# Low parts of block sums on the vector engine, low parts of gate weights by DMA, and all pairs normalized before the first evacuation

## The chip, the cores and the metric

The kernel runs on one core of one Trainium2 chip. Time is device microseconds (us) of that core, from the runs' times; the profile is one further execution with a time of its own. Engines are named as in the profile: PE is the matrix engine (PEld its weight load), DVE the vector engine, ACT the scalar engine, POOL the general engine (it issues the accumulating DMAs), SP the engine that issues the weight loads. Each engine works through its own list of instructions in a fixed order.

## The reference

Two layers over a sequence of 512 positions with 1024 channels, in float32. Layer 0 mixes with a gated convolution and a causal pooling, layer 1 with a spatial gating; each is followed by the same gated ConvFFN, and it is at the start of that FFN, in both layers, that the change lies.

```python
def rms_norm(x, g):
    x32 = x.astype(jnp.float32)
    y = x32 * lax.rsqrt(jnp.mean(x32 * x32, axis=-1, keepdims=True) + EPS)
    return y.astype(x.dtype) * g

def gated_conv_ffn(x, w_gate, w_up, conv_w, conv_b, w_down):
    g = jnp.einsum('bsd,df->bsf', x, w_gate)
    g = causal_dwconv3(g, conv_w) + conv_b
    up = jnp.einsum('bsd,df->bsf', x, w_up)
    return jnp.einsum('bsf,fd->bsd', jax.nn.silu(g) * up, w_down)
...
        hn = rms_norm(h, norm_ffn[layer])
        h = h + gated_conv_ffn(hn, w_ffn_gate[layer], w_ffn_up[layer], conv_ffn[layer],
                               b_conv_ffn[layer], w_ffn_down[layer])
```

The hidden width is 2816, that is 22 columns of 128; the convolution is causal and three wide.

## The kernel before, in words

*Arithmetic.* Every float32 operand of a product is split into a high part that PE takes (float32r) and a low part, the rest. A product is three matmuls into one PSUM bank (`mm3`, lines 134 to 137): high by high, high by low, low by high. A high part is a copy on ACT. A low part is made in one of two ways: `parts` (127 to 132) subtracts on DVE; `summed` (118 to 125) writes the negated high part on ACT, and a DMA issued by POOL adds the source to it (lines 122 to 124).

*Layout.* The residual h lies transposed: eight blocks of 128 channels by 512 positions (`h[0]` to `h[7]`), and beside it `hg`, a high and a low part of each block, the moving operand of the FFN. `PAIRS` sets the order in which the blocks are used: 0, 4, 1, 5, 2, 6, 3, 7. Pair kp is the blocks kp and kp + 4.

*The FFN's groups.* `Ffn.hidden` goes through the 22 columns two at a time; I call two columns a group. The first group (f = 0, `direct`) multiplies with `hg` as it was before normalization (only scaled by the gain), since the norm's root isn't known yet; its results are multiplied by the root r later, in its evacuation. While PE works on it, r becomes known (`rstd_tokens`, `rstd_spread`), and `normalize(kp)` rewrites `hg` for one pair at a time:

- x (line 571, DVE): both blocks of h times gain times r;
- the high parts (575, ACT) and low parts (576, DVE) of the two blocks of hg;
- t (583 to 586, DVE, 256 wide): four block sums of x, which the later groups need for their seven products;
- the split of t into high and low in two halves (590 to 593), by the way of `summed`: ACT, POOL's DMA, ACT.

x and t take turns in three buffers of one tag ("sum"); a buffer is free when all readers of its tile are done, DMAs among them. The weight sums of the later groups (s23, s14) use the same three.

The second group (f = 2, also `direct`) uses the normalized hg: first both gate columns over the eight blocks, then both up columns. From the third group (f = 4, `seven`) on, the up part is seven half-wide products of block sums (line 660, tiles ua, ue, ub) between the gate products (g). Line 617 splits its weight sums.

*Evacuation.* The first group's evacuation (`evacuate`, 547 to 562) multiplies the gate by r on DVE (555), does the convolution (504 on ACT, 506 twice on DVE), silu on ACT (512), a product with r on POOL (558), the product with the up part on DVE (561) and the split of the result (261, 263).

*Loads.* Weights come through four raw buffers in turn (tag "raw", 512 KB each); SP issues the next load when the buffer's last readers are done. The parts have five buffers each (tags "whi", "wlo"), and a buffer is rewritten when PE has used it.

*What sets the order.* The program is written in the order of `hidden`: for the first group, the group's own matmuls, then `pair_weights` of the second group, `normalize` of pairs 0 to 2, the evacuation (`rest`), and `normalize` of pair 3 (lines 717 to 723). A scheduler then places the instructions of each engine by this order and by its own estimate of when operands are ready, so neighbours on an engine may be interleaved. The lists of all engines are fixed when the kernel is built.

Of the kernel before, what the change touches and what calls it, by code (L numbers as in the profile page):

```python
# [15 lines left out]
P = 128  # L16
# [14 lines left out]
def tile_trunk(ctx: ExitStack, tc: tile.TileContext, x, norm_mix, norm_ffn, final_norm,  # L31
# [95 lines left out]
    def parts(raw, a, b, name):  # L127
        hi = wp.tile([P, a, b], F32R, tag="whi", bufs=5, name=f"whi_{name}")
        lo = wp.tile([P, a, b], F32R, tag="wlo", bufs=5, name=f"wlo_{name}")
        nc.scalar.activation(hi, raw, AF.Copy)  # L130
        nc.vector.tensor_tensor(lo, raw, hi.bitcast(F32), ALU.subtract)  # L131
        return hi, lo
# [344 lines left out]
    NP = NK // 2  # L477
# [9 lines left out]
    class Ffn:  # L487
# [27 lines left out]
        def act(self, ft, s):  # L515
            self.acts[ft] = split(self.ap, s, f"a{self.layer}_{ft}", tag="a", bufs=6)

        def pair_weights(self, f, order):

            ch = {}  # L520
            for key, half in order:
                name = f"{key}{self.layer}_{f}_{half}"
                raw = wp.tile([P, 4, 2 * P], F32, tag="raw", bufs=4, name=f"raw_{name}")
                w = (w_ffn_gate if key == "g" else w_ffn_up)[self.layer][:, f * P : (f + 2) * P]
                w = w.rearrange("(h k p) c -> p h k c", h=2, p=P)
                for h_ in range(2):
                    nc.sync.dma_start(raw.rearrange("p (k h) c -> p h k c", h=2)[:, h_],
                                      w[:, h_, 2 * half : 2 * half + 2])
                ch[key, half] = parts(raw, 4, 2 * P, name)
            return ch  # L530

        def direct(self, f, normed, sets, ch, before=lambda i, j: None):
# [33 lines left out]
        def normalize(self, kp):  # L566

            n, r = f"{self.layer}_{kp}", self.r
            x = self.ap.tile([P, 2, S], F32, tag="sum", bufs=3, name=f"x{n}")
            for i, k in enumerate((kp, kp + NP)):  # L570
                nc.vector.scalar_tensor_tensor(x[:, i, :], h[k], self.prm("ffn", k), r,
                                               op0=ALU.mult, op1=ALU.mult)

            def halves(dst, src):
                nc.scalar.activation(dst[0], src, AF.Copy)
                nc.vector.tensor_tensor(dst[1], src, dst[0].bitcast(F32), ALU.subtract)

            halves(hg[kp], x[:, 0, :])
            halves(hg[kp + NP], x[:, 1, :])
            b11, b12 = x[:, 0, :HALF], x[:, 0, HALF:]  # L580
            b21, b22 = x[:, 1, :HALF], x[:, 1, HALF:]
            t = self.ap.tile([P, 4, HALF], F32, tag="sum", bufs=3, name=f"t{n}")
            nc.vector.tensor_tensor(t[:, 1, :], b22, b12, ALU.subtract)
            nc.vector.tensor_tensor(t[:, 0, :], t[:, 1, :], b11, ALU.add)
            nc.vector.tensor_tensor(t[:, 3, :], b12, b11, ALU.subtract)
            nc.vector.tensor_tensor(t[:, 2, :], b21, t[:, 0, :], ALU.subtract)
            self.t23[kp] = self.sums(kp)
            t41 = self.ap.tile([P, 2, 2, HALF], F32R, name=f"t41_{n}")
            self.t41[kp] = t41[:, 0], t41[:, 1]
            for (hi, lo), src in ((self.t23[kp], t[:, :2, :]), (self.t41[kp], t[:, 2:, :])):  # L590
                nc.scalar.activation(lo, src, AF.Copy, scale=-1.0)
                nc.gpsimd.dma_start(lo, src, accum_op=ALU.add)
                nc.scalar.activation(hi, src, AF.Copy)
# [114 lines left out]
        def hidden(self, f, before=lambda i, j: None):  # L708
            if f == 0:
                def first(i, j):  # L710
                    before(i, j)
                    if (i, j) == (1, 0):
                        self.norm.rstd_tokens()
                    elif (i, j) == (2, 2):
                        self.r = self.norm.rstd_spread()

                ch = self.pair_weights(0, [("g", 0), ("u", 0), ("g", 1), ("u", 1)])
                rest = self.direct(0, False, (range(4),), ch, first)
                self.ch = self.pair_weights(2, [("g", 0), ("g", 1), ("u", 0), ("u", 1)])
                for kp in range(NP - 1):  # L720
                    self.normalize(kp)
                rest()
                self.normalize(NP - 1)
            elif f == 2:
                self.direct(2, True, ((0, 1), (2, 3)), self.ch)()
            else:
                self.seven(f)
# [264 lines left out]
```

## Time and profile before

| | |
|---|---|
| time, median of 3 runs | 1026.82 us (1026.61 to 1027.18) |
| profiled execution: its own time | 1027.26 us |
| its span | 1025.5 us |
| mean granted PE clock | 0.993 |
| PE busy | 1005.2 us, 98% |
| DVE busy | 611.0 us, 60% |
| ACT busy | 472.2 us, 46% |
| POOL busy | 91.8 us, 9% |

The span runs from the first to the last instruction; the execution's own time has 1.8 us around it. A line of a timeline gives start, duration, engine, line of the code, operation, output and inputs, and in brackets the idle time of the engine before it with what ended it. Instructions of one engine overlap at their ends, so the distance of two starts, not the duration, says what one more of a kind costs. PEclk is the share of its full clock that PE was granted.

### The profile page before, as it was taken

The page shows a single profiled execution, that of the slowest core. Times are in us where ns is not written, and L with a number is a line of the kernel's source. Part 1 is how long each engine was busy: PE and PEld are TensorE (multiplying, and loading weights), DVE is VectorE, ACT ScalarE, POOL GpSimd, SP SyncE. Part 2 cuts the span into 40 slices and gives each one's busy share as a digit, 9 for nine tenths or more (in the row PEclk, how much of TensorE's full clock was granted, in tenths as well). Part 3 has the DMA queues.
Part 4 walks back from the last instruction along what each step waited for, and adds up shares of the span by engine and source line. Part 5 has one row for each costly group of instructions (what it writes and reads, how often), then busy time and mean ns, then how long its engine had stood idle before and what let it go on. Part 6 is the DMA issues. An engine that isn't in the chain of part 4 may idle for free.

```text
span 1025.5 us, 13018 instructions
## 1 busy us (share of the span) xinstructions
PE 1005.2 (98%) x5169; PEld 857.4 (84%) x5169; DVE 611.0 (60%) x878; ACT 472.2 (46%) x689; POOL 91.8 (9%) x105
## 2 busy tenths in 40 slices
PE   9999999899999999999999999989999999999996
PEld 6788888688898889889888888878889988998885
DVE  5997556855556455636833645486645564664566
ACT  5423435641544246336655443575424632660553
POOL 3141121200000000000300001121000000000000
PEclk9999999899999999999999999999999999999999
DMA  7432234452444343524343223254425343543432
GB/s 228 157 103 82 83 107 106 117 142 64 126 127 138 82 124 116 150 64 139 117 136 103 67 98 94 72 123 106 144 64 139 108 140 82 139 118 93 120 87 82
DMA packets 79881, 114.99 MB, mean 112 GB/s; under 512 B 4069, under 2 KB 53453, under 8 KB 79821
## 3 DMA queue, kind: packets, MB, share of 16 engines
q1 hardware_dynamic: 73580, 98.96, 31.0%
q0 software_dynamic: 4896, 13.63, 7.4%
q10 hardware_dynamic: 1344, 1.58, 0.5%
q8 instruction: 40, 0.66, 0.3%
q14 instruction: 21, 0.16, 0.0%
HBM read 98.42 MB, written 2.10 MB: 98 GB/s over the span
## 4 chain that ended last, share of the span: by engine, by line
PE 92%; DVE 3%; ACT 2%; DMA 1%; issue 1%; POOL 0%; DVEq 0%; ACTq 0%; POOLq 0%
PE ua L660 10%; PE g L136 6%; PE g L135 6%; PE g L137 6%; PE ue L660 5%; PE d L136 4%; PE d L137 4%; PE d L135 4%; PE dn L136 4%; PE dn L137 4%; PE dn L135 4%; PE ub L660 3%; PE gu L136 2%; PE gu L137 2%; PE gu L135 2%; PE v L135 1%
## 5 line engine op out<-in xcount | busy, mean ns | idle before, releaser
L135 PE MATMUL g<-hgh,whi_g 128*128 128x512 f32 x288 | 112.5, 391 | 0.0
L136 PE MATMUL g<-hgl,whi_g 128*128 128x512 f32 x288 | 112.5, 391 | 0.0
L137 PE MATMUL g<-hgh,wlo_g 128*128 128x512 f32 x288 | 112.1, 389 | 0.0
L130 ACT ACTIVATE whi_g<-raw_g 128x1024 fp32r<-128x1024 f32 x44 | 46.3, 1053 | 93.6 <-PE dn L137 57.3
L131 DVE TENSOR_TENSOR wlo_g<-raw_g,whi_g 128x1024 fp32r<-128x1024 f32 x44 | 53.7, 1221 | 28.3 <-ACT whi_g L130 28.3
L136 PE MATMUL d<-a_lo,whi_d 128*128 128x512 f32 x176 | 68.6, 390 | 0.0
L135 PE MATMUL dn<-whi_dn,a_hi 128*128 128x512 f32 x176 | 68.6, 390 | 0.0
L136 PE MATMUL dn<-wlo_dn,a_hi 128*128 128x512 f32 x176 | 68.5, 389 | 0.0
L137 PE MATMUL d<-a_hi,wlo_d 128*128 128x512 f32 x176 | 68.5, 389 | 0.0
L137 PE MATMUL dn<-whi_dn,a_lo 128*128 128x512 f32 x176 | 68.3, 389 | 0.0
L135 PE MATMUL d<-a_hi,whi_d 128*128 128x512 f32 x176 | 68.3, 390 | 0.0
L123 POOL DMA_DIRECT2D wlo_u<-raw_u x18 | 15.4, 857 | 547.3 <-ACT wlo_u L122 261.5
L506 DVE SCALAR_TENSOR_TENSOR c<-rows,prm,c 128x512 f32<-128x512 f32 x88 | 63.7, 747 | 0.7
L137 PEld LDWEIGHTS g<-hgh,wlo_g 128*128 128x128 f32 x288 | 54.1, 188 | 11.9 <-DVE wlo_g L131 0.5
L135 PEld LDWEIGHTS g<-hgh,whi_g 128*128 128x128 f32 x288 | 54.2, 188 | 10.3
L136 PEld LDWEIGHTS g<-hgl,whi_g 128*128 128x128 f32 x288 | 54.2, 188 | 9.8
L617 DVE TENSOR_TENSOR wlo_a<-raw_u,whi_a 128x512 fp32r<-128x512 f32 x18 | 12.4, 691 | 82.1 <-ACT whi_a L616 82.1
L678 ACT COPY kept<-ua 128x256 f32<-128x256 f32 x54 | 19.8, 367 | 77.9 <-PE ua L660 77.9
L131 DVE TENSOR_TENSOR wlo_dn<-raw_dn,whi_dn 128x1024 fp32r<-128x1024 f32 x22 | 26.9, 1223 | 37.0 <-ACT whi_dn L130 37.0
L131 DVE TENSOR_TENSOR wlo_d<-raw_d,whi_d 128x1024 fp32r<-128x1024 f32 x22 | 26.9, 1222 | 37.0 <-ACT whi_d L130 37.0
L616 ACT ACTIVATE whi_s<-s 128x1024 fp32r<-128x1024 f32 x36 | 38.1, 1058 | 22.9 <-PE d L136 14.2
L921 DVE TENSOR_TENSOR y<-dn,y 128x512 f32<-128x512 f32 x32 | 22.1, 690 | 42.9 <-PE dn L137 42.9
(319 smaller groups left out, 2763.0 us busy)
## 6 DMA issues: line engine op xcount, KB each, us to landing
raw_u<-in_w_ffn_up_dram SPq DMA_DIRECT2D x36, 512.0 KB
raw_g<-in_w_ffn_gate_dram SPq DMA_DIRECT2D x36, 512.0 KB
raw_d<-in_w_ffn_down_dram SPq DMA_DIRECT2D x22, 512.0 KB
raw_dn<-in_w_ffn_down_dram SPq DMA_DIRECT2D x22, 512.0 KB
wlo_u<-raw_u POOLq DMA_DIRECT2D x18, 512.0 KB, 4.5
raw_oe<-in_w_out_even_dram SPq DMA_DIRECT2D x8, 512.0 KB
raw_g<-in_w_ffn_gate_dram SPq DMA_DIRECT2D x16, 256.0 KB
raw_u<-in_w_ffn_up_dram SPq DMA_DIRECT2D x16, 256.0 KB
```

Of the source, the lines that this page charges most:

```text
L123: nc.gpsimd.dma_start(lo, raw, accum_op=ALU.add)
L130: nc.scalar.activation(hi, raw, AF.Copy)
L131: nc.vector.tensor_tensor(lo, raw, hi.bitcast(F32), ALU.subtract)
L135: nc.tensor.matmul(ps, lhs[0], rhs[0], start=start, stop=False)
L136: nc.tensor.matmul(ps, lhs[0], rhs[1], start=False, stop=False)
L137: nc.tensor.matmul(ps, lhs[1], rhs[0], start=False, stop=stop)
L506: nc.vector.scalar_tensor_tensor(c, t[:, i : S + i], prm("cf", i * NF + ft), c, op0=ALU.mult, op1=ALU.add)
L616: nc.scalar.activation(hi, src, AF.Copy)
L617: nc.vector.tensor_tensor(lo, src, hi.bitcast(F32), ALU.subtract)
L660: nc.tensor.matmul(ps, l, r, start=at not in opened, stop=end, skip_group_check=True)
L678: nc.scalar.copy(kept[:, i, :], ps)
L921: nc.vector.tensor_tensor(dst, ps, dst, ALU.add)
```

## The change

Three edits, all in the start of an FFN, so each acts twice (once in each layer):

- `pair_weights` can take the way of `summed` for chosen keys; for the second group's gate weights it does. Their low parts are now made by ACT and a POOL DMA and no longer by DVE.
- `normalize` splits the block sums t of pairs 0 and 1 with `halves`: ACT copies, DVE subtracts. Pairs 2 and 3 keep the DMA.
- all four pairs are normalized before the first group's evacuation, instead of three before and one behind.

```diff
-        def pair_weights(self, f, order):
+        def pair_weights(self, f, order, by_dma=""):
...
-                ch[key, half] = parts(raw, 4, 2 * P, name)
+                ch[key, half] = (summed if key in by_dma else parts)(raw, 4, 2 * P, name)
...
             for (hi, lo), src in ((self.t23[kp], t[:, :2, :]), (self.t41[kp], t[:, 2:, :])):
+                if kp < 2:
+                    halves((hi, lo), src)
+                    continue
                 nc.scalar.activation(lo, src, AF.Copy, scale=-1.0)
                 nc.gpsimd.dma_start(lo, src, accum_op=ALU.add)
                 nc.scalar.activation(hi, src, AF.Copy)
...
-                self.ch = self.pair_weights(2, [("g", 0), ("g", 1), ("u", 0), ("u", 1)])
-                for kp in range(NP - 1):
+                self.ch = self.pair_weights(2, [("g", 0), ("g", 1), ("u", 0), ("u", 1)], "g")
+                for kp in range(NP):
                     self.normalize(kp)
                 rest()
-                self.normalize(NP - 1)
```

## The prediction

> **What bounds the kernel now.** I read the page first: the share of each engine, then the chain that ended last.
>
> ```profile
> span 1025.5 us, 13018 instructions
> PE 1005.2 (98%) x5169; PEld 857.4 (84%) x5169; DVE 611.0 (60%) x878; ACT 472.2 (46%) x689; POOL 91.8 (9%) x105
> PE 92%; DVE 3%; ACT 2%; DMA 1%; issue 1%; POOL 0%; DVEq 0%; ACTq 0%; POOLq 0%
> ```
>
> TensorE is busy 98% of the span and owns 92% of the chain. So time can be won only where PE stands still or runs slowly, and anything won there moves everything behind it forward. The timeline of PE around the start of each FFN shows such a place in each layer (columns: start, duration, then in brackets the idle time before and its releaser).
>
> ```profile
> 172.27 0.39 PE L135 MATMUL gu<-hgh,whi_g 128*128 128x512 f32 x1
> ...
> 180.20 0.39 PE L137 MATMUL gu<-hgh,wlo_g 128*128 128x512 f32 x1
> 182.54 0.50 PE L135 MATMUL gu<-hgh,whi_g 128*128 128x512 f32 x1 [1.95 <-ACT hgh L575]
> 185.77 0.79 PE L136 MATMUL gu<-hgl,whi_g 128*128 128x512 f32 x1 [2.73 <-DVE hgl L576]
> 186.37 0.63 PE L137 MATMUL gu<-hgh,wlo_g 128*128 128x512 f32 x1
> ...
> 201.89 0.28 PE L660 MATMUL ua<-hgh,whi_a 128*128 128x256 f32 x1
> ...
> 680.40 0.39 PE L135 MATMUL gu<-hgh,whi_g 128*128 128x512 f32 x1
> ...
> 690.29 0.50 PE L135 MATMUL gu<-hgh,whi_g 128*128 128x512 f32 x1 [1.58 <-ACT hgh L575]
> 693.54 0.80 PE L136 MATMUL gu<-hgl,whi_g 128*128 128x512 f32 x1 [2.74 <-DVE hgl L576]
> ...
> 708.40 0.28 PE L660 MATMUL ua<-hgh,whi_a 128*128 128x256 f32 x1
> ```
>
> 172.27 and 680.40 are the first matmuls of the second group (columns 2 and 3 of the FFN). From 172.27 to 180.20 lie 35 steps, 7.93 us: 0.2266 us a matmul. The group has 2 sets x 8 blocks x 2 columns x 3 = 96 matmuls, so without a stop it takes 21.76 us; it takes 201.89 - 172.27 = 29.62 us in layer 0 and 708.40 - 680.40 = 28.00 us in layer 1. The loss is **7.86 us + 6.24 us = 14.10 us**. The stop comes after 36 matmuls, six of the eight blocks, at 172.27 + 36 x 0.2266 = 180.43: what is missing is block 3, normalized by the last pair, first its high part from ACT, then its low part from DVE. PE stands 182.54 - 180.43 = 2.11 and 185.77 - 182.77 = 3.00 us, and in layer 1 by the same count 1.73 and 3.02 us. The rest of the loss, 2.75 and 1.49 us, is matmuls at a lower clock behind the stop (0.63 us each at 186.37 instead of 0.39); the granted clock of the two stretches says the same:
>
> ```profile
> 172.27:201.89 29.62, 24.94 (x97) 19.85 (x96) 25.47 (x41) 20.62 (x33) 7.43 (x7) 0.88 0.51 115
> 680.40:708.40 28.00, 23.68 (x97) 18.99 (x96) 25.02 (x40) 20.52 (x33) 7.45 (x7) 0.94 0.50 110
> ```
>
> The fields after PE, PEld, DVE, ACT and POOL are clock (0.88, 0.94), DMA share and GB/s. DVE and ACT are busy under 90% of these stretches. Why the last pair is late is in DVE's timeline:
>
> ```profile
> 158.10 1.42 DVE L571 SCALAR_TENSOR_TENSOR x<-h,prm,rstd_f 128x512 f32<-128x512 f32 x2 [4.09 <-ACT rstd_f L222]
> 159.43 0.42 DVE L585 TENSOR_TENSOR t<-x 128x256 f32<-128x256 f32 x1
> 159.77 1.29 DVE L576 TENSOR_TENSOR hgl<-x,hgh 128x512 fp32r<-128x512 f32 x2
> 160.97 0.42 DVE L583 TENSOR_TENSOR t<-x 128x256 f32<-128x256 f32 x1
> 161.31 1.22 DVE L131 TENSOR_TENSOR wlo_g<-raw_g,whi_g 128x1024 fp32r<-128x1024 f32 x1
> 162.44 0.42 DVE L584 TENSOR_TENSOR t<-t,x 128x256 f32<-128x256 f32 x1
> ...
> 171.75 0.75 DVE L571 SCALAR_TENSOR_TENSOR x<-h,prm,rstd_f 128x512 f32<-128x512 f32 x1 [3.88 <-DMA t<-t]
> ...
> 179.74 0.74 DVE L571 SCALAR_TENSOR_TENSOR x<-h,prm,rstd_f 128x512 f32<-128x512 f32 x1
> ...
> 183.98 0.69 DVE L561 TENSOR_TENSOR s<-gu,s 128x512 f32<-128x512 f32 x1 [1.17 <-POOL s L558]
> 184.59 1.74 DVE L576 TENSOR_TENSOR hgl<-x,hgh 128x512 fp32r<-128x512 f32 x2
> ```
>
> Two causes. Pair 2's x (171.75) waits 3.88 us for a DMA: x and t share three buffers, and pair 0's t is held until the accumulating DMA that reads it lands. And pair 3's x (179.74) and low parts (184.59) stand between the steps of the first evacuation, behind a product that waits for POOL.
>
> **The change, part by part.** The built order of the changed kernel has PE and SP as before; DVE, ACT and POOL differ only from here to the start of the third group, in both layers.
>
> *Pairs 0 and 1: low parts of the block sums on DVE.* Four DVE subtractions a layer are added. Starts give the pitch of an operation: 0.67 for a 512-wide x (two from 158.10 to 159.43), 0.60 for a subtraction (159.77 to 160.97), 0.34 for 256 wide, 1.13 for 1024 wide (161.31 to 162.44). So +4 x 0.60 = 2.40 us of DVE. Gone are four DMAs and their issues, four ACT copies, and the 3.88 us wait, as t of pair 0 is free when DVE has read it.
>
> *Gate low parts by DMA.* DVE loses 2 x 1.13 = 2.26 us, ACT gains two 1024-wide copies, POOL two issues, each DMA moving as much as two of the four removed.
>
> ```profile
> 160.09 1.05 ACT L130 ACTIVATE whi_g<-raw_g 128x1024 fp32r<-128x1024 f32 x1
> ...
> 178.10 0.62 ACT L591 ACTIVATE t<-t 128x512 fp32r<-128x512 f32 x1
> 178.62 0.62 ACT L593 ACTIVATE t<-t 128x512 fp32r<-128x512 f32 x1
> ...
> 179.94 1.28 ACT L512 ACT_TABLE_LOAD   x1
> 181.24 0.72 ACT L512 ACTIVATE s<-c,prm 128x512 f32<-128x512 f32 x1
> ```
>
> ACT: about +2 x 1.05 - 4 x 0.52 = 0. The engines' sums stay level; what changes is the order.
>
> *Order.* All of pair 3 now stands ahead of the second step of the evacuation. On DVE there are, from 158.10 to the low part of block 3: eight x (5.32), fourteen 256-wide (4.70), ten subtractions 512 wide (6.00), two up-weight low parts (2.26) and one evacuation product (512 wide, 0.60): 18.88 us, if nothing waits. So it starts at 176.98 and ends at **177.58**. PE wants it one matmul after 180.43, at 180.66: 3.1 us of room, and block 7's (178.18) has more. On ACT the high part stands behind a weight half whose buffer PE frees at the end of the first group (172.27), then four copies of pair 2's t. The last two wait for DVE's t, done 2.61 us before 176.98 (two x, two 256-wide and the evacuation product follow it), at 174.37; they start behind the first two near 174.9, end near 175.9 at 0.52 each (178.10 to 178.62), and the high part of block 3 at about 176.5, 3.9 us ahead. So both stops go, and with them the slow stretch.
>
> *The DMAs of the gate weights.* The timeline of ACT, POOL and SP has these starts:
>
> ```profile
> 150.07 0.61 ACT L187 ACTIVATE last_f<-h 128x512 f32<-128x512 f32 x1
> ...
> 163.85 1.01 POOL L592 DMA_DIRECT2D t23l<-t  x1 [14.75 <-ACT t23l L591]
> 165.31 0.87 POOL L592 DMA_DIRECT2D t<-t  x1 [0.45 <-ACT t L591]
> ...
> 176.83 0.86 POOL L592 DMA_DIRECT2D t23l<-t  x1 [2.18 <-ACT t23l L591]
> ...
> 182.05 3.12 POOL L558 TENSOR_TENSOR s<-s,rstd_f 128x512 f32<-128x512 f32 x2 [2.17 <-ACT s L512]
> ...
> 164.02 13.94 SPq L112 DMA_DIRECT2D raw_g<-in_w_ffn_gate_dram  x2
> ```
>
> and the view of DMA issues gives the time from issue to landing (last number) of three of them:
>
> ```profile
> t<-t POOLq DMA_DIRECT2D x1, 256.0 KB, 6.3
> ...
> t23l<-t POOLq DMA_DIRECT2D x1, 256.0 KB, 4.1
> ...
> wlo_u<-raw_u POOLq DMA_DIRECT2D x1, 512.0 KB, 4.5
> ```
>
> 6.3 is the DMA issued at 165.31, 4.1 the one at 176.83, 4.5 one of the third group, of 512 KB. The second DMA starts after two copies from 160.09, near 162.1. A DMA of this very size took 4.5; the worst of half the size 6.3, issued at 165.31 among weight loads; twice that, 12.6, is my upper bound. I take 4.5 (same size): it lands at 166.6, at worst 174.7. PE wants it at the third block, 172.27 + 24 x 0.2266 = 177.71. Hidden by at least 3 us. The first follows a copy behind the norm's last square (150.07), near 151.8; it lands by 156.3, at worst 164.4, wanted at 172.5. On SP the load of the next up half waits for it, and behind that load three more: the first gate load of the third group waits for the second DMA (landing 166.6 to 174.7) where it waited for DVE until 164.02. Its ACT copy comes after the six blocks' matmuls free a buffer, near 177.8: no cost, unless both the DMA and the load take their worst. In layer 1 the first copy also stands ahead of one residual copy and the norm's root on ACT. Between 0 and its own 0.95 us I take 0, since the spread that needs the root has a fixed place in PE's order behind 24 matmuls of the first group.
>
> *What is late next.* The third group starts 7.86 us earlier, at 194.03. Its first wants on DVE are the low parts of its gate weights: the second half at 194.03, a product of 12 matmuls of half the width (1.36) and 6 of full width (1.36) on: 196.75. Ahead of it: table load to about 182.05, silu (0.65), POOL's product (1.9: it starts at 182.05 and releases DVE at 183.98), DVE product and conv step, the second silu and POOL product, to about 188.5, then seven DVE steps (0.60, 0.66, 0.60, 0.60, 0.66, 1.13, 1.13 = 5.4): 193.9. Room 2.8 us. Cost 0, but it is the thinnest cover.
>
> **Sum.** -14.10 us, nothing added. Against the profiled execution (1027.26, span 1025.5) that is 1013.2; the median of the runs shown, 1026.82, lies 0.44 under that execution: 1012.7. I say **1013.0**.
>
> **Rivals.**
> *A part of the stop stays, or comes back in the third group.* If the steps on POOL take longer, the 2.8 us of room go. For: two subtractions beside POOL's products took 1.74 (at 184.59) against 1.29 (159.77), and the changed order puts conv steps, which read two tensors from SBUF, beside them. Were both products twice as long, +3.8 us, PE would stop 1.0 us a layer: about 1015; with 1 us more and a slow stretch as today's (2.75 and 1.49 us) about 1021. Against: DVE's 18.88 us have no wait in them that I find.
>
> The Trainium skill, "SBUF — State Buffer", section "Who interferes with whom", would have it worse: a DVE instruction with two SBUF inputs and a GpSimd instruction that reads SBUF block each other fully. The trace has 1.74 for 1.29, a partial loss for two. By that rule this rival, about 1015, is what happens; by the row the products cost nothing more than they do now.
>
> *Slower: the gate DMA does not land while DVE is packed.* If POOL's DMA moved only in DVE's gaps, DVE's new order has none from 158.10 to about 184.4 (eleven steps, 6.8 us, behind 177.58), where it waits for POOL; the second gate DMA would land 4.5 later, at 188.9, and PE stop 11.2 us from 177.71. With today's slow stretches that is 13.9 us for 7.86 and 12.7 for 6.24: 12.5 us slower in all, 1039. It decides from a stop of 5.1 us, a landing at 182.8. Against it: the DMA issued at 176.83 landed in 4.1 us, in a stretch in which DVE was busy all the time (5.00 of 5.00):
>
> ```profile
> 175.00:180.00 5.00, 5.00 (x24) 4.14 (x23) 5.00 (x9) 4.98 (x10) 1.71 (x2) 1.00 0.69 98
> ```
>
> *The order helps nothing:* the last pair still comes at its old time, since a wait I overlooked (a shared buffer, the load ahead of ACT's copy) takes the place of the DMA's. Then 1027. Against: up to pair 3 each of the three buffers is released by earlier instructions of DVE and ACT themselves; the only DMAs left that hold one are those of pair 2, and the third group's sums alone want that buffer.
>
> **How the numbers follow.** Forecast 0.76; part of it 0.13; slower 0.08; no change 0.03. Faster is 0.76 + 0.13 = 0.89. 0.2% is 2 us, about what this kernel's measurement can tell from no change. The range: at the low end the whole loss plus the spread of the runs, 1011.0; at the high end most of the first rival, 1018.0.
>
> **What would show it.** Right: no PE idle by hgh or hgl in the second group, 21.8 us from its first matmul to the third group's, at clock 1.00, in both layers; the last low parts on DVE about 19 us after the first x; x of pair 2 without a wait; no PE wait at the third group's gates. Wrong: PE waiting for the gates' DMA, for a low part in the third group, or for hgl again.

## The result, and the profile after

The changed kernel takes **1013.29 us** (1012.43 to 1014.56) where the kernel before took 1027.0 us (1026.61 to 1029.09) beside it: a ratio of 0.986, with a 95% interval of 0.985 to 0.988, so 13.7 us faster. The prediction was 1013.0. The profiled execution took 1013.46 us.

The page of the changed kernel, its span, its engines and the chain that ended last:

```profile
span 1011.5 us, 13009 instructions
PE 998.6 (99%) x5169; PEld 853.3 (84%) x5169; DVE 612.6 (61%) x882; ACT 471.5 (47%) x685; POOL 90.0 (9%) x101
PE 95%; DVE 3%; ACT 1%; issue 1%; DMA 1%; POOL 0%; DVEq 0%; ACTq 0%; POOLq 0%
```

PE has the same 5169 matmuls and 6.6 us less of busy time: the matmuls that ran at the lower clock. Its share of the chain went from 92% to 95%. Beside the rows of the kernel before stand now the two stretches of the second group, from its first matmul to the first one of the third group, in layer 0 and in layer 1 (stretch, its length, busy time of PE, PEld, DVE, ACT and POOL with counts, granted clock, DMA share, GB/s):

```profile
171.21:192.97 21.76, 21.76 (x97) 18.02 (x96) 21.76 (x34) 17.54 (x27) 6.98 (x6) 1.00 0.49 113
672.98:694.78 21.80, 21.80 (x98) 18.02 (x97) 21.80 (x34) 17.58 (x27) 6.96 (x6) 1.00 0.50 116
```

29.62 and 28.00 us have become 21.76 and 21.80: 7.86 and 6.20 us, at a clock of 1.00 instead of 0.88 and 0.94, and PE is busy from end to end. What PE still waits for, over the whole run (us in total, times, longest), is here:

```profile
PE wst L764 <- POOL ws L757: 1.5, 1, 1.5
PE clock L56 <- DVE idle L53: 1.3, 1, 1.3
PE z L135 <- ACT hgh L382: 1.0, 2, 0.8
PE z L136 <- DVE hgl L384: 0.8, 1, 0.8
PE xt_ps L371 <- DMA xt<-in_x_dram: 0.7, 1, 0.7
```

No wait of the second or third group is left. In the kernel before the same view begins with 5.5 and 3.5 us for the two parts of hg:

```profile
PE gu L136 <- DVE hgl L576: 5.5, 2, 2.7
PE gu L135 <- ACT hgh L575: 3.5, 2, 1.9
...
```

The first row of after is new: the transposes of the spatial weights, between the layers, wait 1.5 us for a select on POOL. DVE's timeline shows the last pair and what follows it:

```profile
157.04 1.41 DVE L571 SCALAR_TENSOR_TENSOR x<-h,prm,rstd_f 128x512 f32<-128x512 f32 x2 [4.10 <-ACT rstd_f L222]
...
173.34 1.41 DVE L571 SCALAR_TENSOR_TENSOR x<-h,prm,rstd_f 128x512 f32<-128x512 f32 x2
...
175.94 1.29 DVE L576 TENSOR_TENSOR hgl<-x,hgh 128x512 fp32r<-128x512 f32 x2
...
182.07 0.69 DVE L633 TENSOR_TENSOR s<-raw_u 128x512 f32<-128x512 f32 x1
182.68 1.79 DVE L506 SCALAR_TENSOR_TENSOR c<-rows,prm,c 128x512 f32<-128x512 f32 x1
184.39 0.68 DVE L561 TENSOR_TENSOR s<-gu,s 128x512 f32<-128x512 f32 x1
...
186.91 1.78 DVE L506 SCALAR_TENSOR_TENSOR c<-rows,prm,c 128x512 f32<-128x512 f32 x1
...
192.88 1.21 DVE L131 TENSOR_TENSOR wlo_g<-raw_g,whi_g 128x1024 fp32r<-128x1024 f32 x1
```

From the first x (157.04) to the first low part of the last pair (175.94) are 18.90 us, with no bracket on the way: DVE never waited. In the kernel before the same distance was 184.59 - 158.10 = 26.49 us.

### The profile page after: what moved, and what is told of

Read it like the earlier page. It is cut to its first block, busy times and chain, and to the rows that moved or that the text cites. A ratio compares the mean times of both kernels' runs of the same rounds, so it can differ in the third digit from the quotient of the medians.

```text
span 1011.5 us, 13009 instructions
## 1 busy us (share of the span) xinstructions
PE 998.6 (99%) x5169; PEld 853.3 (84%) x5169; DVE 612.6 (61%) x882; ACT 471.5 (47%) x685; POOL 90.0 (9%) x101
## 3 DMA queue, kind: packets, MB, share of 16 engines
q10 hardware_dynamic: 1344, 1.58, 0.5%
## 4 chain that ended last, share of the span: by engine, by line
PE 95%; DVE 3%; ACT 1%; issue 1%; DMA 1%; POOL 0%; DVEq 0%; ACTq 0%; POOLq 0%
PE ua L663 10%; PE g L135 7%; PE g L136 6%; PE g L137 6%; PE ue L663 5%; PE d L136 4%; PE dn L137 4%; PE dn L135 4%; PE d L137 4%; PE d L135 4%; PE dn L136 4%; PE gu L135 3%; PE gu L137 3%; PE gu L136 3%; PE ub L663 3%; PE u L135 1%
## 5 line engine op out<-in xcount | busy, mean ns | idle before, releaser
L130 ACT ACTIVATE whi_g<-raw_g 128x1024 fp32r<-128x1024 f32 x40 | 42.1, 1053 | 93.6 <-PE dn L137 57.3
L506 DVE SCALAR_TENSOR_TENSOR c<-rows,prm,c 128x512 f32<-128x512 f32 x88 | 68.1, 793 | 0.6
L131 DVE TENSOR_TENSOR wlo_g<-raw_g,whi_g 128x1024 fp32r<-128x1024 f32 x40 | 48.8, 1221 | 28.3 <-ACT whi_g L130 28.3
```

What stands on the lines that cost most here:

```text
L506: nc.vector.scalar_tensor_tensor(c, t[:, i : S + i], prm("cf", i * NF + ft), c, op0=ALU.mult, op1=ALU.add)
```

## The experiments

Theory: PE stops in the second group because the low part of the last pair comes after the instant at which PE wants it, and that goes once the low part stands ahead of the evacuation's wait for POOL. Rivals: that one of the three edits is the real cause and the others idle; and that the third group takes the loss over.

One yardstick for all kernels is counted in layer 0 and layer 1 from starts in the timelines: from the first x on DVE to the first matmul of the third group (the first "ua"), and from there to the first product "ue", which measures the third group's first part. Times are medians; each ratio is to the kernel before, run beside it.

| kernel | time, us | ratio (95%) | x to ua, L0 / L1 | ua to ue, L0 / L1 |
|---|---|---|---|---|
| before | 1027.0 | 1 | 43.79 / 42.17 | 15.23 / 15.24 |
| after | 1013.29 | 0.9863 (0.9846 to 0.9880) | 35.93 / 35.93 | 15.24 / 15.23 |
| order and halves | 1012.56 | 0.9859 (0.9845 to 0.9874) | 35.93 / 35.94 | 15.23 / 15.23 |
| halves and gate DMA | 1012.66 | 0.9861 (0.9846 to 0.9876) | 35.93 / 35.93 | 15.23 / 15.24 |
| order and gate DMA | 1016.42 | 0.9899 (0.9883 to 0.9916) | 36.07 / 36.44 | 17.06 / 17.09 |
| order only | 1015.87 | 0.9891 (0.9876 to 0.9906) | 36.62 / 35.93 | 16.62 / 16.60 |
| halves only | 1015.22 | 0.9890 (0.9866 to 0.9913) | 36.28 / 36.28 | 16.47 / 16.43 |
| gate DMA only | 1015.06 | 0.9890 (0.9871 to 0.9908) | 36.69 / 37.57 | 15.23 / 15.23 |
| last x 5 times | 1016.85 | 0.9906 (0.9888 to 0.9925) | 36.36 / 36.35 | 17.09 / 17.12 |
| last x 7 times | 1022.67 | 0.9968 (0.9957 to 0.9980) | 36.29 / 36.32 | 20.80 / 19.37 |

35.93 and 15.23 are these stretches without a stop.

### Two of the three edits

*Order and halves: the gate low parts on DVE again.*

```diff
-                self.ch = self.pair_weights(2, [("g", 0), ("g", 1), ("u", 0), ("u", 1)], "g")
+                self.ch = self.pair_weights(2, [("g", 0), ("g", 1), ("u", 0), ("u", 1)])
```

> All pairs before the evacuation and DVE splits for pairs 0 and 1, but the gate weights' low parts stay on DVE. Counted from the first x on DVE: PE needs the low part of block 3 at 22.6 us; the changed kernel has it at 19.5. Theory (only the queue on DVE decides, and it has room): one 1024-wide subtraction (1.13) more ahead of it, 20.6, still in time: no PE idle in the second group, 1013 to 1014.5. Rival (the gate DMA is what buys the time): the second group or the third group's gates stop again, 1 us or more a layer, 1015.5 or more.

Measured: 1012.56 us. The low parts start at 178.25 and the first x at 158.22, so block 3's ends 20.63 us behind it. The gate DMAs aren't needed beside the other two edits: the 2.26 us that they take off DVE are covered by the room.

*Halves and gate DMA: the last pair behind the evacuation again.*

```diff
-                for kp in range(NP):
+                for kp in range(NP - 1):
                     self.normalize(kp)
                 rest()
+                self.normalize(NP - 1)
```

> DVE splits for pairs 0 and 1 and the gate weights by DMA, but pair 3 is again normalized behind the evacuation in the program. In the order that the scheduler then builds, two evacuation products and four conv steps stand ahead of block 3's low part, and the evacuation's product with the up part behind it. Theory (the place in DVE's queue decides, not the order of the program): low part at 16.3 + 1.2 + 1.33 + 2.64 + 0.6 = 22.1 us from the first x, needed at 22.6: at most 0.5 us of stop a layer, 1013 to 1016. Rival (normalizing pair 3 ahead of the evacuation is what does it): the stop of 5.1 and 4.8 us with its slow clock is back, 1025 to 1027.

Measured: 1012.66 us. The low part of block 3 ends 178.65 + 0.60 - 157.17 = 22.08 us behind the first x, as the theory had it. The written order isn't needed either: with pair 2 no longer held by a DMA, the scheduler by itself puts the last pair's low part ahead of the product that waits for POOL (182.13).

*Order and gate DMA: the block sums of pairs 0 and 1 through the DMA again.*

```diff
-                if kp < 2:
-                    halves((hi, lo), src)
-                    continue
```

> All pairs before the evacuation and the gate low parts by DMA, but the block sums of pairs 0 and 1 by DMA as before. The DMA of pair 0's sums stands behind that of the gate weights on POOL's queue. Theory: x of pair 2 waits until 9.5 to 13 us from the first x (reached at 8.9), x of pair 3 until about 16 to 17, low part of block 3 at 20 to 21.5, needed at 22.6: no stop, 1013 to 1015. Rival (six DMAs queue up behind each other and hold the buffers): a stop of 2 us or more a layer, 1018 or more.

Measured: 1016.42 us, 1.4 above the theory's range and 1.6 below the rival's. There is no stop of 2 us in the second group, but the theory overlooked the third. DVE waits again for the DMA that holds t (3.20 us at 170.89 and 1.69 us at 174.89), and what it does later is late in the third group, where PE waits 1.2 us in each layer for the low part of the gate weights.

### One edit alone

The edits are those above, the other two undone in each.

> All pairs before the evacuation, nothing else: block sums by DMA, gate low parts on DVE. x of pair 2 waits again for pair 0's DMA (13.6 us from the first x), x of pair 3 for pair 1's DMA (about 19). Theory: low part of block 3 near 22.9, needed at 22.6: a stop of 0.3 to 1 us a layer and the third group's gates late by about 1: 1014 to 1018. Rival (the DMA wait is the cause, and without removing it the order helps little): x of pair 3 comes as late as before, 1023 or more.

> One part alone: block sums of pairs 0 and 1 split on DVE; gate low parts on DVE, pair 3 behind the evacuation in the program. Theory (DVE's queue and its waits): one 1024-wide subtraction (1.13) more ahead of block 3's low part than with the gate DMA, where it ended 22.1 us after the first x; so 23.2, needed at 22.6: a stop of about 0.65 us a layer, perhaps 0.5 in the third group: 1013.5 to 1016. Rival (at least two of the three parts are needed): the stop is 2 us or more a layer, 1017 or more.

> One part alone: gate low parts by DMA; block sums of pairs 0 and 1 by DMA, pair 3 behind the evacuation in the program. Theory: the waits for the DMAs of pairs 0 and 1 stay (x of pair 3 at 17.7 us from the first x, as with the new order), then low part at about 22.8 of 22.6 and the third group's gates late by 0.5 to 1.5: 1013.5 to 1018. Rival (at least two of the three parts are needed): a stop of 2 us or more a layer, 1019 or more.

Measured: 1015.87, 1015.22 and 1015.06 us, each in its theory's range. By the ratios each alone gives about 11 of the 14 us, so the rivals, by which one edit alone helps little, fall. With the order alone DVE's wait for the DMA is still there, in the timeline of that kernel:

```profile
170.84 0.75 DVE L571 SCALAR_TENSOR_TENSOR x<-h,prm,rstd_f 128x512 f32<-128x512 f32 x1 [3.86 <-DMA t<-t]
...
179.58 1.28 DVE L576 TENSOR_TENSOR hgl<-x,hgh 128x512 fp32r<-128x512 f32 x2
```

and PE's stops at hg shrink from 5.5 and 3.5 us to 0.4 us, with a new one at the third group's gate weights:

```profile
...
PE g L137 <- DVE wlo_g L131: 1.5, 2, 0.7
...
PE gu L136 <- DVE hgl L576: 0.4, 1, 0.4
```

So of the prediction's two causes, the 3.88 us wait for a DMA isn't what stopped PE by itself: it stays, and most of the stop goes. What every one of these kernels has and the kernel before hasn't is the low part ahead of the product behind POOL.

How long PE stops at hg follows from the distance between the first x and the end of block 3's low part, which PE wants after 180.66 - 158.10 = 22.56 us. With the order alone it ends after 22.96 us in layer 0, with the gate DMA alone after 23.05 and 23.92 us (layers 0 and 1): 0.40, 0.49 and 1.36 us late. The idle times of PE there are these, from the one kernel and then from the other:

```profile
180.31 0.50 PE L136 MATMUL gu<-hgl,whi_g 128*128 128x512 f32 x1 [0.38 <-DVE hgl L576]
```

```profile
181.16 0.50 PE L136 MATMUL gu<-hgl,whi_g 128*128 128x512 f32 x1 [0.47 <-DVE hgl L576]
...
682.84 0.50 PE L136 MATMUL gu<-hgl,whi_g 128*128 128x512 f32 x1 [1.34 <-DVE hgl L576]
```

The 0.8 to 2.1 us a layer that each still loses lie where DVE is late next: with the order alone and the halves alone mostly at the third group's gate weights, with the gate DMA alone at hg itself. Halves together with either other edit leave no such loss.

### How much room there is

The last pair's x is computed five or seven times instead of once, each time into the same buffer:

```diff
+                for _ in range(5 if kp == NP - 1 else 1):
                     nc.vector.scalar_tensor_tensor(x[:, i, :], h[k], self.prm("ffn", k), r,
                                                    op0=ALU.mult, op1=ALU.mult)
```

> The changed kernel with both x of pair 3 computed five times over (eight more steps of 0.67 on DVE a layer, 5.3 us; same result). Block 3's low part comes at 24.85 us of 22.56: a stop of 2.3 us in the second group, and the third group's gates (1.75 us of room before) stop for 1.3 us more: 3.6 us a layer. Theory A (a stop under about 3 us keeps the clock): 1013.3 + 7.2 = 1020.5. Theory B (any stop of 2 us brings the slow stretch of 1.5 to 2.75 us): 1023.5 to 1026.

> The same with both x of pair 3 seven times over (twelve more steps, 8.0 us a layer). Stop of 4.95 us in the second group, in one piece or two, and 1.3 us in the third: 6.25 us a layer, 1025.8 without a slow stretch. Both theories of the clock expect the slow stretch here, 1.5 to 2.75 us a layer: 1028.8 to 1031.3. If DVE had slack somewhere behind, less than 1025.

Measured: 1016.85 and 1022.67 us, both less than theories A and B gave; the second is also under the 1025 that stood for slack somewhere behind. The rows say where the delay went. In both kernels DVE does the additional work (five times, then seven times):

```profile
173.72 6.71 DVE L572 SCALAR_TENSOR_TENSOR x<-h,prm,rstd_f 128x512 f32<-128x512 f32 x10
...
180.68 1.28 DVE L577 TENSOR_TENSOR hgl<-x,hgh 128x512 fp32r<-128x512 f32 x2
```

```profile
173.96 9.36 DVE L572 SCALAR_TENSOR_TENSOR x<-h,prm,rstd_f 128x512 f32<-128x512 f32 x14
...
183.58 1.28 DVE L577 TENSOR_TENSOR hgl<-x,hgh 128x512 fp32r<-128x512 f32 x2
```

6.71 - 1.41 = 5.30 and 9.36 - 1.41 = 7.95 us are added. But the scheduler knows of it, and gives PE other matmuls first. With five times, PE's order in the second group becomes this:

```profile
179.97 0.39 PE L136 MATMUL gu<-hgl,whi_u 128*128 128x512 f32 x1
180.48 0.73 PE L135 MATMUL gu<-hgh,whi_g 128*128 128x512 f32 x2
181.05 0.39 PE L137 MATMUL gu<-hgh,wlo_u 128*128 128x512 f32 x1
```

The up columns (whi_u) come ahead of the last gate blocks. So the low part ends 180.68 + 0.60 - 157.42 = 23.86 us behind the first x, where the old order of PE wanted it after 22.56, and still the second group loses 0.4 us only. The rest of DVE's delay goes to the third group. By the table the two stretches together lose 2.29 and 2.31 us (layers 0 and 1) for 5.30 us of work, so about 3.0 us were covered; for 7.95 us they lose 5.93 and 4.53 us. The layer that loses 4.53 has no slow matmuls (below), so 3.4 us were covered there. (The time rose by 3.56 and 9.38 us, 1.0 and 1.1 less than these losses: the 1.5 us wait of the changed kernel at the spatial weights isn't there.) That is near the rooms that the prediction counted, 3.1 and 2.8 us, but these were counted for another order of PE, so the nearness may be chance. Both theories failed in the assumption that PE's order stays: the loss comes out in the third group and not where they put it.

The run with seven times also bears on what a stop does to the clock. In layer 0 its third group has stops of 1.20, 1.60 and 0.46 us, and the stretch behind the second one runs at a clock of 0.73:

```profile
198.23 0.50 PE L135 MATMUL g<-hgh,whi_g 128*128 128x512 f32 x1 [1.20 <-ACT whi_g L130]
...
201.25 0.39 PE L664 MATMUL ua<-t23h,wlo_s 128*128 128x256 f32 x1 [1.60 <-DVE wlo_s L621]
203.18 0.58 PE L664 MATMUL ua<-t23h,whi_s 128*128 128x256 f32 x1 [0.46 <-ACT kept L682]
...
201.25:204.80 3.55, 3.08 (x17) 2.88 (x18) 3.55 (x6) 1.53 (x3) 0.00 (x0) 0.73 0.07 10
204.90:207.50 2.60, 2.60 (x10) 2.10 (x10) 1.66 (x3) 2.13 (x3) 0.00 (x0) 0.73 0.51 180
```

In layer 1 the same kernel has nearly the same stops, and the matmuls behind them keep their pitch (0.39 us each; the granted clock is 1.00 from 707.09 to 713.30):

```profile
704.06 0.50 PE L135 MATMUL g<-hgh,whi_g 128*128 128x512 f32 x1 [1.26 <-ACT whi_g L130]
...
707.09 0.39 PE L664 MATMUL ua<-t,wlo_s 128*128 128x256 f32 x1 [1.58 <-DVE wlo_s L621]
...
709.02 0.50 PE L664 MATMUL ua<-t,whi_s 128*128 128x256 f32 x2 [0.46 <-ACT kept L682]
...
710.42 0.39 PE L135 MATMUL g<-hgh,whi_g 128*128 128x512 f32 x1
```

The slow stretch is why layer 0 loses 1.40 us more. So the clock can fall behind stops of this size, and need not: theory A fails in layer 0, theory B had no stop of 2 us to be tried on, and what else decides is not shown here. The Trainium skill, "TensorE: Matmul & The Clock Gate", section "HAM oscillation — how this bites in real kernels", gives the rule of thumb that gaps over about 3.4 us slow the clock. In layer 0 it fell without such a gap (the longest was 1.60 us), and so it did in the kernel before (the longest was 3.00 us).

### The two at the edges: POOL's product, and the spatial weights

*The product of the gate with r (line 558) on DVE instead of POOL.*

```diff
                     if not normed:
-                        nc.gpsimd.tensor_tensor(s, s, r, ALU.mult)
+                        nc.vector.tensor_tensor(s, s, r, ALU.mult)
```

> The changed kernel with the product of the gate by the row scale (line 558, two per evacuation of a group that is not normalized) on VectorE in place of GpSimd; VectorE gets two products of about 0.68 us more per layer. Theory (GpSimd's product and VectorE's convolution step exclude each other for their whole length): the convolution steps beside it take about 0.66 us each again where the changed kernel had one of 1.7 us twice per layer, so that VectorE as a whole loses nothing by the move (1.36 us more work, some 2.1 us less blocked). Rival (only a partial loss, as the prediction took it): the steps get shorter by 0.45 us each at most and VectorE ends the evacuation later than before. The time is expected within 1.5 us of the changed kernel by either; the durations of the rows decide, and waits of TensorE in the third group show where VectorE is late, since one of the third group's low parts of the gate weights is placed later here.

Measured: 1012.24 us (1012.11 to 1012.26), a ratio of 0.9861 (0.9847 to 0.9876). The group of DVE's convolution steps (least, median and longest duration in ns) in the changed kernel, and then in this one:

```profile
L506 DVE SCALAR_TENSOR_TENSOR c<-rows,prm,c x88: 733/746/1790, 177.5 to 979.4; 128x512 f32<-128x512 f32 x88
```

```profile
L506 DVE SCALAR_TENSOR_TENSOR c<-rows,prm,c x88: 734/746/752, 177.7 to 978.1; 128x512 f32<-128x512 f32 x88
```

The long steps are gone. The 1.05 us less in time has another source: the yardsticks of the FFN are those of the changed kernel (35.93 and 15.23 us), and what is missing is the wait of 1.55 us at the transposes of the spatial weights, which this kernel doesn't have. What the long steps were is told by POOL's rows of the changed kernel, an undisturbed operation first and then the products:

```profile
500.38 1.29 POOL L191 TENSOR_TENSOR ssq_m<-ssq_m,sq_m 128x512 f32<-128x512 f32 x1 [0.84 <-ACT sq_m L190]
```

```profile
181.94 1.98 POOL L558 TENSOR_TENSOR s<-s,rstd_f 128x512 f32<-128x512 f32 x1 [1.50 <-ACT s L512]
186.56 1.58 POOL L558 TENSOR_TENSOR s<-s,rstd_f 128x512 f32<-128x512 f32 x1 [2.65 <-ACT s L512]
```

Another POOL operation of this size took 1.29 us (first row). The product of 181.94 takes 0.69 us more: it stands until DVE's sum of 182.07 is over, and that sum runs at its usual 0.69. Then DVE's step of 182.68 takes 184.39 - 182.68 = 1.71 us instead of 0.66: it stands until about the product's end at 183.92. One is held for the whole of the other, and then the other for the whole of what is left. Of the theories the full lock is right; the partial loss that the prediction took would have left steps of at most 0.66 + 0.45 = 1.11 us.

*The load of the spatial weights ahead of the broadcast.*

```diff
-            nc.scalar.dma_start(g_bc, sgu_norm.rearrange("(o l) d -> o l d", o=1)
-                                .to_broadcast([P, 1, D]))
             ws = mp.tile([P, NK, P], F32, tag="v", bufs=4, name="ws")
             nc.scalar.dma_start(ws, w_spatial[0].rearrange("h t s -> t h s"))
+            nc.scalar.dma_start(g_bc, sgu_norm.rearrange("(o l) d -> o l d", o=1)
+                                .to_broadcast([P, 1, D]))
```

> The changed kernel with one line moved: in the odd mixer the load of the spatial weights is issued ahead of the broadcast load of the gate norm. Theory: the 1.5 us for which TensorE waits at the transposes of the spatial weights (wst after ws, once in the run) is a new loss that the change uncovers there: the select on GpSimd starts when the load lands, and the load is queued behind the broadcast. Then the wait falls below 0.5 us and the time goes down by 1.0 to 1.5 us, to about 1012. Rival: the wait is set by the select itself (1.99 us in the changed kernel, 1.09 before), which takes longer beside VectorE, or by when the buffer is free, and the time moves by less than 0.4 us.

Measured: 1013.08 us (1012.95 to 1013.87), a ratio of 0.9872 (0.9855 to 0.9888): no gain that can be told from the changed kernel, as the rival had it. The timelines of POOL and PE, of the changed kernel and then of this one:

```profile
508.87 1.99 POOL L757 TENSOR_SCALAR_AFFINE_SELECT ws<-ws 128x1024 f32<-128x1024 f32 x1 [2.81 <-DMA ws<-in_w_spatial_dram]
...
510.92 0.66 PE L764 MATMUL wst<-ident,ws 128*128 128x128 f32 x4 [1.55 <-POOL ws L757]
```

```profile
506.47 1.31 POOL L757 TENSOR_SCALAR_AFFINE_SELECT ws<-ws 128x1024 f32<-128x1024 f32 x1 [0.20 <-DMA ws<-in_w_spatial_dram]
...
507.84 0.66 PE L764 MATMUL wst<-ident,ws 128*128 128x128 f32 x4 [0.97 <-POOL ws L757]
```

The select starts 2.40 us earlier, yet PE still waits 0.97 us: the scheduler, which expects the load earlier, has put the transposes earlier in PE's order too, behind 20 matmuls of that mixer instead of 32. The theory took the place of the transposes as fixed; it follows the scheduler's estimate, and so an earlier load alone didn't remove the wait.

The length of the select, on which the rival rested, is a matter of the same lock. In the kernel before, POOL's select comes first:

```profile
517.11 1.09 POOL L755 TENSOR_SCALAR_AFFINE_SELECT ws<-ws 128x1024 f32<-128x1024 f32 x1 [2.14 <-DMA ws<-in_w_spatial_dram]
```

DVE's subtraction of two tensors (line 131, 128x1024) starts 0.46 us behind it and takes 1.71 us instead of 1.21. In the changed kernel that subtraction starts at 508.69, 0.18 us ahead of the select, and takes its usual 1.23; the select now takes 1.99, that is 0.90 more. So 0.90 of the 1.55 us that PE waits here are the lock, from a lag of 0.18 us; the rest goes with the load, which landed about 5.6 us behind its issue instead of 4.9.

*Both: order and halves, with this load first.*

> Order and low parts on VectorE kept, gate weights' low parts on VectorE again instead of by DMA, and the spatial weights loaded ahead of the broadcast. Theory: the gains add: 1012.56 of the version with the gate low parts on VectorE, less what the moved load gives in the run beside this one where that version waits at the transposes too; 1011.0 to 1012.6. Rival: without the DMAs the load is issued no earlier and the wait at the transposes isn't there, so that the time stays at 1012.4 to 1013.

Measured: 1012.88 us (1012.55 to 1013.17), 0.9868 (0.9853 to 0.9882). That is in the rival's range and above the theory's, but not by the rival's mechanism: without the load moved, this version had no wait at the transposes at all, and with it PE waits 1.0 us there. Among after and the three versions from 1012.2 to 1012.7 us none is shown to be the fastest: their intervals overlap over most of their length.

## Why the prediction was right

*What bounds, and the sum.* The loss of 14.10 us in the second group was the whole gain: the two stretches lost 7.86 + 6.20 = 14.06 us, stops and slow clock together. By PE's first matmul of the third group the kernel is 201.89 - 192.97 = 8.92 us ahead in layer 0, of which 172.27 - 171.21 = 1.06 were there when the second group began. They arise in the first 12 us of the run, far ahead of the first instruction that the change touches: after 7.78 the matmuls of the kernel before start about 0.43 us apart until about 10, those of the changed kernel are at 0.23 from 8.9 on. The kernels with order and halves and with the gate DMA alone start as slowly as the kernel before (first x at 158.22 and 157.98, beside 158.10 before and 157.04 after), so none of the three edits brings this lead. Between the layers 1.58 us are given back: the transposes of the spatial weights were at 518.26 before and are at 510.92, 7.34 us ahead instead of 8.92. So the predicted sum, 1013.2 against the profiled execution, met 1013.46 with two small terms that it didn't have. The term of 14.10 was right; that the other two nearly cancel is luck.

*The last pair.* Predicted: block 3's low part starts 18.88 us behind the first x and ends after 19.48. Measured: 18.90, and 19.5 by the pitch of 0.60. The high part on ACT:

```profile
174.89 1.14 ACT L575 ACTIVATE hgh<-x 128x512 fp32r<-128x512 f32 x2
```

holds two copies of about 0.5 us; the first, block 3's, starts 17.85 us behind the first x and ends near 18.4, as predicted (176.5 - 158.10). Pair 2's x runs without a wait.

*The gate DMAs.* Rows of POOL and of the DMA issues:

```profile
150.89 1.01 POOL L123 DMA_DIRECT2D wlo_g<-raw_g  x1 [2.86 <-ACT wlo_g L122]
...
161.33 0.87 POOL L123 DMA_DIRECT2D wlo_g<-raw_g  x1 [9.43 <-DVE t L584]
```

```profile
wlo_g<-raw_g POOLq DMA_DIRECT2D x1, 512.0 KB, 4.7
...
wlo_g<-raw_g POOLq DMA_DIRECT2D x1, 512.0 KB, 6.1
```

They land 4.7 and 6.1 us after issue; 4.5 was assumed. The second is there at 161.33 + 6.1 = 167.4, and PE wants it at 171.21 + 24 x 0.2266 = 176.65: hidden by 9 us. DVE was busy all the time from 161.33 to the landing, and in layer 1 as well (5.17 of 5.17 us, landing after 5.1), so the rival that forecast a slower kernel falls. (The first DMA says nothing on this: DVE was busy for only 0.83 of its 4.7 us.) One row was misread on the way: the prediction's worst DMA of half the size took 6.3 us, but the one of 163.85 in the same trace took 6.5, which would make its upper bound 13.0 instead of 12.6. That part of the change cost nothing and, beside the other two, brought nothing.

*The rival on the third group, and the thinnest cover.* This step was mis-sized, without a cost in time. Predicted: the second half of the third group's gate low part is ready 0.13 us before the third group starts, a room of 2.8 us. Measured: it is ready at 192.88 + 1.13 = 194.01, 1.04 us after the start (192.97), so the room is 1.7 us. The prediction let the convolution steps beside POOL's products cost their normal 0.66 us; each of the two costs 1.71. DVE goes on at 184.39 and 188.62, 0.47 and 0.48 us behind the ends of POOL's products (183.92 and 188.14) at which the prediction let it go on; that is 0.95 of the 1.17 us by which the operand is later than forecast (193.9 less the 1.06 of the start). The row on which this rested, two subtractions in 1.74 us instead of 1.29, was misread as a partial loss: that pair started at 184.59, when POOL's two products (182.05, 3.12 us) had 0.58 us left to run, so a full block ending at 185.17 explains it as well. The rule of the Trainium skill, "SBUF — State Buffer", section "Who interferes with whom", that a DVE instruction with two SBUF inputs and a GpSimd instruction that reads SBUF block each other fully, agrees with the rows here. The prediction had put it at 1015 us by that rule, from products twice as long and a stop of 1.0 us; but POOL's products took 1.98 and 1.58, and the room left after the locks was still 1.7 us, so no stop came.

*What the prediction didn't see.* It took the three edits for parts of one cure. Each alone would have won 11 to 12 us and two suffice for all, if one of them is the halves of pairs 0 and 1. And the lists of the engines follow the scheduler's estimate, so the same edit also moved other work: that was covered by the built order for this change, but not where a delay was added by experiment.

## What to carry to other kernels

A stop of a busy engine that costs 6 to 8 us, the slow matmuls behind it included, can hang on the place of one 0.6 us instruction in another engine's list: look first for what stands ahead of the late operand there, above all a step that waits for a third engine, before removing work. When a stop goes, count the room of the next operand as well, since a delay that the first stage hides comes out in the next: here 5.30 us more on DVE cost 0.4 us in the second group and 1.9 us in the third. With a scheduler, each edit moves the other engines' lists, PE's too, so take the want from the built order and not from the old one.

## What the runs showed of the hardware that wasn't expected

- A POOL product and a two-input DVE step hold each other up completely: 1.71 us instead of 0.66 on DVE, 1.98 instead of 1.29 on POOL. With the product on DVE (0.69 us), no convolution step of 88 is longer than 752 ns. So the two products on an otherwise idle POOL cost DVE 2 x 1.05 us a layer, more than the 2 x 0.60 us that they take on DVE itself.
- PE's clock fell to 0.73 behind stops of 1.20 and 1.60 us that end 3.0 us apart, and in the other layer of the same kernel it stayed at 1.00 behind stops of 1.26 and 1.58 us that end as far apart. A stop's length alone doesn't tell whether the clock falls.
- The same select on POOL (128 x 1024) took 1.09 us where it started ahead of DVE's two-input subtraction and 1.99 us where it started 0.18 us behind it; in the first case the subtraction took 1.71 us instead of 1.21. Whichever starts first runs at its usual length, and the other is held.
